# One transposing transfer for both 16-bit planes of a tile, and other due times for the weights' transfers

## The chip, the cores and the metric

The kernel runs on one core of a Trainium2 chip. Its time is the device time of the program in microseconds. Before the change it is 1276.15 us, the median of three runs (1275.52 to 1277.26).

## What is computed

Two layers of a hybrid block over 272 tokens (16 learned ones and 256 of the input) with 1024 features, all in fp32, and a norm at the end:

```python
for li in range(DEPTH):
    h = h + mixer(rms_norm(h, norm_mix_g[li]), w_in[li], w_branch[li], w_out[li], ...)
    h = h + conv_ffn(rms_norm(h, norm_ffn_g[li]), w_ffn_in[li], ...)
h = rms_norm(h, norm_final_g)

def mixer(hn, ...):
    proj = hn @ w_in                      # 1024 -> 13312 columns, split into 12 parts
    o_ret = retention(rq, rk, rv, rg)     # 4 heads, keys of 128, values of 256
    o_hg = hgrn2(hq, hf, hi, hg)          # 8 heads, gated linear recurrence
    o_da = diff_attention(dq, dk, dv)     # 8 heads, difference of two softmaxes
    y = sum(sigmoid(gate_n) * (branch_n @ w_branch[n]) for n in range(3))
    return y @ w_out
```

The padding of 112 positions that the reference puts ahead is left out by the kernel, since no valid token sees it.

## The kernel before, in words

**Products.** Activations lie with features on partitions and tokens along the row. Every weight tile of 128x128 is the stationary operand, the tokens are the moving one. For the precision of fp32 each weight tile is split into two parts, whi and wlo, and each activation into hi and lo, and three matmuls add up (L953 to L955): whi with hi, whi with lo, wlo with hi. The text calls these three one product. Parts of three outputs that are cut like this are also the operands of the heads (L1062 to L1064).

**Weights.** `_Weights.next` (L642 on) brings them in chunks of eight tiles, 512 KB: a transfer on SP's queue into `wraw` (three buffers), a copy on ACT into `whi` and a subtraction on DVE into `wlo` (four buffers each). The copy and the subtraction carry a due time, the moment at which the first product of the chunk is planned; the transfer has none.

**Turns.** Values, the maps of attention, some tails and, at the end, the residual are needed with tokens on partitions. `to_tokens`, `flip`, `da_rest` and `residual` do it without TensorE: ACT copies the upper and the lower 16 bits of each number into two planes (`apart`, for `flip` the first half of `turned`), SP issues a transposing transfer for each plane (`turned`), and ACT copies the two planes back together. A plane has one block of 128 columns in `flip`, three in `da_rest`, four in the others.

**The heads.** Retention (`ret_head`, tiles s, ro), the recurrence (`hg_heads`, `hg_outputs`, tiles lev, ho) and attention (`da_first`, `da_pair`, `da_rest`, `da_tail`, tiles ds, do) run beside the products of other parts: each is a chain over DVE, ACT, SP, GpSimd and back to TensorE. Their results on TensorE lie in two accumulators (tag "acc"). Such an accumulator comes free when the head's norm has been taken: a square on ACT, a sum over the partitions on GpSimd, a root in two steps on ACT, a multiplication on DVE.

**Order.** Every operation is recorded first (`_Engine.__getattr__`, L633 is the line of all of them), with an estimate of its cost and a key, the time at which it is wanted. `_Plan.order` then simulates the engines and writes down in which order each of them does its work; on the chip that order is fixed. At each step an engine takes the operation that can start first, and among those that can start at once the one with the lowest rank (L498 to L506): an operation whose due time is less than URGENT (3 us) behind the product that TensorE has reached goes ahead of all others, else the key decides. A transposing transfer counts as 0.06 us, plus its bytes at 360 GB/s, plus 0.7 us, and lands 2 us later.

Of the kernel before, what the change touches and what calls it, by code (L numbers as in the profile page):

```python
# [21 lines left out]
P = 128  # L22
# [17 lines left out]
SLOTS = 13  # L40
# [8 lines left out]
HOLD, PULL = 3.0, 8.0  # L49
SAFE = 1.0  # L50
SURE = 0.3
URGENT = 3


BASE = {"rq": 0, "rk": 4, "rv": 8, "rg": 16, "hq": 24, "hf": 32, "hi": 40, "hg": 48,
# [300 lines left out]
class _Plan:  # L356
# [99 lines left out]
    def order(self):  # L456
# [11 lines left out]
        held, out = set(), []  # L468
# [29 lines left out]
        def rank(op, t):  # L498
            if op.engine == "pe" and op not in mains:
                if op.fed + SAFE > t:  # L500
                    return math.inf
                return op.key - PULL if beside and op.fed + SURE <= t else op.key + HOLD
            if op.due - reached < URGENT:
                return op.due - 1000.0
            late = 8.0 if op.func in self.SETS and self.SETS[op.func] != tables else 0.0
            return op.key + late  # L506
# [4 lines left out]
        while len(out) < todo:  # L511
# [53 lines left out]
            for o in op.after:  # L565
                o.need -= 1
                if o.engine != e:
                    o.fed = max(o.fed, done + self.LAG[e])
                o.ready = max(o.ready, done + (self.LAG if o.engine != e else self.SAME)[e])
                if o.need == 0:  # L570
                    push(o)
            for o in op.then:
# [20 lines left out]
class _Engine:  # L593
# [5 lines left out]
    def __getattr__(self, method):  # L599
        f = getattr(self.engine, method)  # L600

        def call(*args, **kw):
# [20 lines left out]
            if method == "reciprocal":  # L623
                cost += 7 * self.each * n
            elif method == "tensor_tensor_scan":
                cost += self.each * n
            elif method == "transpose":
                cost = 0.11
            elif method == "matmul":
                cost = max(0.218 if args[1].shape[-1] > 32 else 0.07, 4 * n / 2400 + 0.02)  # L630
            elif method == "dma_start":
                cost = self.fixed + self.each * n * outs[0].shape[0] + (0.7 if kw.get("transpose") else 0.0)
            self.plan.add(self.name, lambda: f(*args, **kw), cost, outs, ins, kind)  # L633

        return call
# [2 lines left out]
class _Weights:  # L638
# [13 lines left out]
    def next(self):  # L652
        c, i = divmod(self.used, CHUNK_TILES)
        self.used += 1
        if i == 0:
            due = self.plan.key
            room = [P, ROOM]
            raw = self.plan.tile(self.pool, [P, CHUNK_TILES * P], F32, "wraw", 3, f"wraw{c}")
            hi = self.plan.tile(self.pool, room, F32R, "whi", 4, f"whi{c}")
            lo = self.plan.tile(self.pool, room, F32R, "wlo", 4, f"wlo{c}")  # L660
            self.plan.key = due - LEAD
            pieces = 1 if c > 1 else 2
            for p in range(pieces):
                n = CHUNK_TILES // pieces
                cols = slice(p * n * P, (p + 1) * n * P)
                self.sp.dma_start(raw[:, cols], self.w[c][:, cols])
                order, places = self.places[c]
                mine = [[x[i] for i in order[p * n : (p + 1) * n]] for x in places]
                for first, outer, inner, dims in _boxes(*mine):
                    src = self.part(raw, (p * n + first) * P, inner * P, P, outer, inner)  # L670
                    to_hi, to_lo = (self.part(t, *x, outer, inner) for t, x in zip((hi, lo), dims))
                    self.act.activation(to_hi, src, AF.Copy)
                    self.dve.tensor_tensor(out=to_lo, in0=src, in1=to_hi.bitcast(F32), op=SUB)
                    for op in self.plan.ops[-2:]:
                        op.due = due
            self.plan.key = due
            self.cut = hi, lo
        return tuple(t[:, at[i] : at[i] + P] for t, at in zip(self.cut, self.places[c][1]))
# [16 lines left out]
def _trace(ctx, tc, plan, a, depth, probe):  # L695
# [298 lines left out]
    def planes(name, n):  # L994
        return new(tp, [P, 4 * T], U16, "vsrc", 4, name)[:, : 2 * n].rearrange("p (i x) -> p i x", i=2)

    def to_tokens(src, vt, e):

        apart, turned = planes("apart", 4 * P), planes("turned", 4 * P)
# [2 lines left out]
        for i in range(2):  # L1002
            act.activation(apart[:, i].rearrange("p (c f x) -> p c f x", c=2, f=2),
                           halves(src[:, :, : 2 * P], i).rearrange("p f (c x) -> p c f x", c=2), AF.Copy)
        for i in range(2):
            sync.dma_start(turned[:, i].rearrange("p (b x) -> p b x", x=P), apart[:, i], transpose=True)
        turned = turned.rearrange("p i (c x) -> p i c x", c=2)
        if top is None:
            for i in range(2):
# [10 lines left out]
    def flip(out, x):  # L1020
# [3 lines left out]
        halves = lambda t, i: t.bitcast(U16).rearrange("p (x two) -> p x two", two=2)[:, :, i]  # L1024
        for i in range(2):
            act.activation(apart[:, i], halves(x, i), AF.Copy)
        for i in range(2):
            sync.dma_start(turned[:, i].rearrange("p (b x) -> p b x", x=P), apart[:, i], transpose=True)
        for i in range(2):
            act.activation(halves(out, i), turned[:, i], AF.Copy)  # L1030

# [46 lines left out]
    for li in range(depth):  # L1078
# [365 lines left out]
        def da_rest(b, hd, sb, nm, sm, cf, tiles):  # L1444
# [17 lines left out]
            for i in range(2):  # L1462
                for c, n, at in ((0, 2 * P, P), (T, P, 0)):
                    act.activation(apart[:, i, at : at + n], halves(w[:, c : c + n], i), AF.Copy)
            for i in range(2):
                sync.dma_start(turned[:, i].rearrange("p (b x) -> p b x", x=P), apart[:, i], transpose=True)
            for i in range(2):
                act.activation(halves(a1[:, META : T + P], i), turned[:, i], AF.Copy)

# [73 lines left out]
        def residual():  # L1543
# [5 lines left out]
            for g, (t, c) in enumerate(((0, 0), (0, 1), (1, 0))):  # L1549
                apart, turned = planes("apart", 4 * P), planes("turned", 4 * P)  # L1550
                halves = lambda x, i: x.bitcast(U16).rearrange("p k (x two) -> p k x two", two=2)[:, :, :, i]
                for i in range(2):
                    act.activation(apart[:, i].rearrange("p (k x) -> p k x", k=4), halves(h[:, 4 * c : 4 * c + 4, META + t * P : META + (t + 1) * P], i), AF.Copy)
                for i in range(2):
                    sync.dma_start(turned[:, i].rearrange("p (b x) -> p b x", x=P), apart[:, i], transpose=True)
                for i in range(2):
                    act.activation(halves(st["old"][:, g : g + 1], i), turned[:, i].unsqueeze(1), AF.Copy)
                plan.key += 20.0
# [250 lines left out]
```

## Time and profile before

| | |
|---|---|
| median of three runs | 1276.15 us |
| the profiled execution | 1276.58 us |
| its span, first to last instruction | 1274.8 us |
| TensorE busy | 1261.6 us |
| VectorE (DVE), ScalarE (ACT), GpSimd (POOL) busy | 964.8, 899.2, 115.5 us |
| weights' transfers on SP's queue | 402 of 512 KB and 4 of 256 KB |
| transposing transfers on SP's queue | 86 and 36 |

The profile is of one execution. TensorE's matmuls (PE) and weight loads (PEld) have rows of their own; SPq, ACTq and so on are the engines' sequencers, and an SPq row of a transfer is the time that SP needs to issue it, not that of the data. Releasers, in rows as `<-DVE wlo`, are inferred from semaphores: what came last before a waiting instruction could start. The parts of the program in order of time: the first layer's projections with the recurrence to about 200 us, retention to 262, attention with the three branches to 455, the feed-forward part to 651; the second layer the same way to the end.

### The profile page before, as it was taken

To read this page: it belongs to the slowest core of one execution; us is meant where nothing else is said; L and a number is where in the kernel's file an instruction comes from. 1 tells how busy PE (TensorE), PEld (TensorE's weight loads), DVE (VectorE), ACT (ScalarE), POOL (GpSimd) and SP (SyncE) were. 2 spreads that over 40 slices of the span, in tenths; PEclk is the share of its full clock that TensorE was granted. 3 is DMA by queue.
4 is the path that set the end of the run, shared out by engine and by line. 5 is a ranking of instruction groups with operands and counts; after the bars stand their busy time and mean duration, and the time that the engine had idled before them with its cause. 6 is when DMAs were issued, how large, how long until landed. Compare 5 with 4: busy or idle time off the path is not lost.

```text
span 1274.8 us, 28782 instructions
## 1 busy us (share of the span) xinstructions
PE 1261.6 (99%) x11612; PEld 1240.7 (97%) x11612; DVE 964.8 (76%) x1677; ACT 899.2 (71%) x1700; POOL 115.5 (9%) x89
## 2 busy tenths in 40 slices
PE   9999999999999999999999999999999999999998
PEld 9999999999999999999999999999999999999986
DVE  6797587899775789886576875878897868898854
ACT  6766687788797576665456567887788975787643
POOL 2000031101111000000010000411012210000000
PEclk9999999999999999999999999999999999999999
DMA  7655557556647546556555546475565566576663
GB/s 269 196 168 155 165 152 216 170 152 190 197 142 207 183 151 198 180 170 193 172 180 180 168 145 190 151 228 174 154 190 176 166 202 203 167 213 205 206 196 110
DMA packets 109205, 230.49 MB, mean 181 GB/s; under 512 B 55312, under 2 KB 55440, under 8 KB 109072
## 3 DMA queue, kind: packets, MB, share of 16 engines
q1 hardware_dynamic: 108784, 228.13, 58.0%
q8 instruction: 91, 1.49, 0.5%
q10 hardware_dynamic: 288, 0.52, 0.1%
q14 instruction: 42, 0.34, 0.1%
HBM read 216.16 MB, written 1.05 MB: 170 GB/s over the span
## 4 chain that ended last, share of the span: by engine, by line
PE 84%; issue 5%; DVE 3%; DMA 3%; ACT 3%; POOL 2%; SPq 0%; ACTq 0%; POOLq 0%; DVEq 0%
PE main L953 24%; PE main L955 24%; PE main L954 24%; DMA wraw<-in_w 3%; POOL hr L633 2%; PE fo L1593 2%; PE fo L1594 2%; PE fo L1595 2%; PE lev L1178 1%; DVE wlo L633 1%; PE fi L955 1%; PE fi L954 1%; PE fi L953 1%; ACT whi L633 1%; PE ds L1422 1%
## 5 line engine op out<-in xcount | busy, mean ns | idle before, releaser
L953 PE MATMUL main<-xh,whi 128*128 128x272 f32 (+1 forms) x2240 | 642.6, 287 | 0.7 <-ACT whi L633 0.7
L633 DVE TENSOR_TENSOR wlo<-wraw,whi 128x1024 fp32r<-128x1024 f32 (+1 forms) x411 | 498.4, 1217 | 188.6 <-ACT whi L633 183.1
L955 PE MATMUL main<-xh,wlo 128*128 128x272 f32 (+1 forms) x2240 | 636.9, 284 | 1.2 <-DVE wlo L633 1.0
L954 PE MATMUL main<-xl,whi 128*128 128x272 f32 (+1 forms) x2240 | 636.1, 284 | 1.0 <-issue 1.0
L633 ACT ACTIVATE whi<-wraw 128x1024 fp32r<-128x1024 f32 (+1 forms) x411 | 426.1, 1041 | 195.2 <-PE main L954 78.5
L955 PEld LDWEIGHTS main<-xh,wlo 128*128 128x128 f32 x2240 | 421.6, 188 | 3.5 <-DVE wlo L633 2.2
L953 PEld LDWEIGHTS main<-xh,whi 128*128 128x128 f32 x2240 | 421.7, 188 | 2.2 <-ACT whi L633 1.2
L954 PEld LDWEIGHTS main<-xl,whi 128*128 128x128 f32 x2240 | 421.7, 188 | 0.2
L633 POOL PARTITION_ALL_REDUCE hr<-hsq x36 | 76.9, 2155 | 426.6 <-ACT hsq L633 388.9
L633 DVE SCALAR_TENSOR_TENSOR two_b<-main,small,two_b 128x256 f32<-128x256 f32 (+2 forms) x128 | 54.6, 487 | 28.3 <-ACT two_b L633 28.2
L633 ACT ACTIVATE two_b<-main,small 128x272 f32<-128x272 f32 (+1 forms) x64 | 33.1, 566 | 28.1 <-PE main L955 28.1
L953 PE MATMUL main<-ghi,whi 128*128 128x272 f32 x176 | 50.8, 289 | 0.0
L954 PE MATMUL main<-glo,whi 128*128 128x272 f32 x176 | 50.6, 287 | 0.0
L955 PE MATMUL main<-ghi,wlo 128*128 128x272 f32 x176 | 50.3, 286 | 0.0
L955 PE MATMUL main<-b1hi,wlo 128*128 128x272 f32 (+1 forms) x128 | 36.6, 286 | 1.2 <-DVE wlo L633 1.2
L953 PE MATMUL main<-b0hi,whi 128*128 128x272 f32 (+1 forms) x128 | 37.3, 291 | 0.2 <-DVE y L633 0.2
L953 PE MATMUL main<-b1hi,whi 128*128 128x272 f32 (+1 forms) x128 | 37.1, 290 | 0.0
L953 PE MATMUL main<-yhi,whi 128*128 128x272 f32 (+1 forms) x128 | 36.4, 284 | 0.0
L955 PE MATMUL main<-yhi,wlo 128*128 128x272 f32 (+1 forms) x128 | 36.3, 284 | 0.0
L954 PE MATMUL main<-b0lo,whi 128*128 128x272 f32 (+1 forms) x128 | 36.3, 284 | 0.0
L954 PE MATMUL main<-b1lo,whi 128*128 128x272 f32 (+1 forms) x128 | 36.3, 284 | 0.0
L954 PE MATMUL main<-ylo,whi 128*128 128x272 f32 (+1 forms) x128 | 36.3, 284 | 0.0
(283 smaller groups left out, 2169.2 us busy)
## 6 DMA issues: line engine op xcount, KB each, us to landing
wraw<-in_w SPq DMA_DIRECT2D x402, 512.0 KB, 3.8
turned<-apart SPq DMA_TRANSPOSE x86, 2.7
h<-in_h SPq DMA_DIRECT2D x4, 272.0 KB, 5.6
dec<-in_dec SPq DMA_DIRECT2D x2, 544.0 KB, 6.1
wraw<-in_w SPq DMA_DIRECT2D x4, 256.0 KB, 5.2
const<-in_const SPq DMA_DIRECT2D x1, 937.0 KB, 5.4
turned<-turned SPq DMA_TRANSPOSE x36, 2.4
gain<-in_gl SPq DMA_DIRECT2D x1, 512.0 KB, 5.0
```

The source lines that it names most:

```text
L633: self.plan.add(self.name, lambda: f(*args, **kw), cost, outs, ins, kind)
L953: nc.tensor.matmul(o, wh, hi, start=first, stop=False)
L954: nc.tensor.matmul(o, wh, lo, start=False, stop=False)
L955: nc.tensor.matmul(o, wl, hi, start=False, stop=last)
L1178: nc.tensor.matmul(o, keys, x, start=True, stop=True)
L1422: nc.tensor.matmul(ss[m][:, at : at + nk], q[half, hd, q0 : q0 + P], k[half, hd, :nk], start=True, stop=True)
L1593: nc.tensor.matmul(o, gh, wh, start=first, stop=False)
L1594: nc.tensor.matmul(o, gl, wh, start=False, stop=False)
L1595: nc.tensor.matmul(o, gh, wl, start=False, stop=end)
```

## The change

1. The two transfers of a turn become one, in a function `turn`: planes and blocks are one list of blocks, twice as long (8, 6 or 2 instead of 4, 3 or 1).
2. The planner counts a turn as 1.3 us, whatever its size, and lets it start no sooner than half a us (STILL) after its planes are written.
3. The weights' transfers get the due time of their chunk (from the 14th on), and URGENT becomes a number for each engine: 4.5 us for ACT, 3 as before for DVE, 12 for SP, where it puts the weights ahead of turns.

```diff
-URGENT = 3
+URGENT = {"act": 4.5, "dve": 3.0, "sp": 12.0}
+TURN = "turn"
+STILL = 0.5
...
-            if op.due - reached < URGENT:
+            if op.due - reached < URGENT.get(op.engine, 0.0):
                 return op.due - 1000.0
...
-                o.ready = max(o.ready, done + (self.LAG if o.engine != e else self.SAME)[e])
+                o.ready = max(o.ready, done + (self.LAG if o.engine != e else self.SAME)[e] + STILL * (o.func == TURN))
...
             elif method == "dma_start":
-                cost = self.fixed + self.each * n * outs[0].shape[0] + (0.7 if kw.get("transpose") else 0.0)
+                cost, kind = (1.3, TURN) if kw.get("transpose") else ( self.fixed + self.each * n * outs[0].shape[0], None)
...
                 self.sp.dma_start(raw[:, cols], self.w[c][:, cols])
+                fetch = self.plan.ops[-1]
...
                     for op in self.plan.ops[-2:]:
                         op.due = due
+                    fetch.due = due if c > SLOTS else math.inf
...
+    def turn(out, x):
+
+        sync.dma_start(out.rearrange("p i (b x) -> p (i b) x", x=P), x.rearrange("p i x -> p (i x)"), transpose=True)
...
-        for i in range(2):
-            sync.dma_start(turned[:, i].rearrange("p (b x) -> p b x", x=P), apart[:, i], transpose=True)
+        turn(turned, apart)
```

The last piece stands in `to_tokens`, `flip`, `da_rest` and `residual`. The order moves on all engines; TensorE does the same matmuls, with the heads' products at other places among the main ones. Three places follow, each before and after.

SP, second layer, the end of attention. The transfers into wraw are weights, turned_1882 is a turn of the last head, turned_1889 that of the tails. Before:

```order
L633 DMA wraw_1999<-in_w 128x1024
L633 DMA wraw_2002<-in_w 128x1024
L633 DMA_TRANSPOSE turned_1882<-apart_1881 128x3x128
L633 DMA_TRANSPOSE turned_1889<-turned_1889 128x1x128 x2
L633 DMA_TRANSPOSE turned_1882<-apart_1881 128x3x128
L633 DMA wraw_2006<-in_w 128x1024
L633 DMA wraw_2009<-in_w 128x1024
```

After:

```order
L635 DMA wraw_1999<-in_w 128x1024
L635 DMA_TRANSPOSE turned_1874<-apart_1873 128x6x128
L635 DMA wraw_2002<-in_w 128x1024
L635 DMA_TRANSPOSE turned_1889<-turned_1889 128x2x128
L635 DMA wraw_2006<-in_w 128x1024
L635 DMA_TRANSPOSE turned_1882<-apart_1881 128x6x128
L635 DMA wraw_2009<-in_w 128x1024
```

Four transfers stood ahead of wraw_2006 behind wraw_2002, now one does; turned_1874, the turn of the head before, has moved down to here.

ACT, second layer, the start of the second half of attention. two_a and two_b are the two maps of a pair of heads (1840 and 1841 of the one, 1842 and 1843 of the other), whi_1960 the split of a chunk of weights. Before, the end of the stretch between the copy wts_1830 and that split:

```order
L633 ACTIVATE two_b_1843,dm_1845<-two_b_1843,dm_1845 128x272
L633 ACTIVATE two_a_1842,dm_1845<-two_a_1842,dm_1845 128x144
L633 ACTIVATE apart_1847<-two_a_1840 128x256
L633 ACTIVATE apart_1847<-two_a_1840 128x128
L633 ACTIVATE apart_1847<-two_a_1840 128x256
L633 ACTIVATE apart_1847<-two_a_1840 128x128
L633 ACTIVATE dt_1834<-two_a_1840 128x16 x2
L633 ACTIVATE m_957_1932<-main_1940 128x2x258
L633 ACTIVATE two_b_1843,dm_1845<-two_b_1843,dm_1845 128x144
L633 ACTIVATE whi_1960<-wraw_1959 128x4x256
```

After:

```order
L635 ACTIVATE whi_1952<-wraw_1951 128x1024
L635 ACTIVATE wts_1830<-turned_1832 128x128
L635 ACTIVATE whi_1960<-wraw_1959 128x4x256
L635 ACTIVATE two_a_1840,dm_1844<-two_a_1840,dm_1844 128x272
L635 ACTIVATE two_b_1841,dm_1844<-two_b_1841,dm_1844 128x272
L635 ACTIVATE two_a_1840,dm_1844<-two_a_1840,dm_1844 128x144
```

The split now stands ahead of all eight exponentials and of the planes (apart_1847).

ACT, first layer, retention. sum_484 and hr_485 are the squares and the root of head 0's norm, tw_473 the tails that its second product waits for, whi_563 and whi_566 splits of weights. Before:

```order
L633 ACTIVATE tw_473<-ro_472 128x128
L633 ACTIVATE whi_554<-wraw_553 128x1024
L633 ACTIVATE kt_490<-wts_489 128x272
L633 ACTIVATE sum_484<-ro_482 128x272
L633 ACTIVATE sum_484<-ro_483 128x272
L633 ACTIVATE whi_563<-wraw_562 128x1024
L633 ACTIVATE vsrc_546<-main_535 128x544
L633 ACTIVATE whi_566<-wraw_565 128x1024
L633 ACTIVATE hr_485<-hr_485,eps_84 128x272
```

After:

```order
L635 ACTIVATE tw_473<-ro_472 128x128
L635 ACTIVATE whi_554<-wraw_553 128x1024
L635 ACTIVATE kt_480<-wts_479 128x272
L635 ACTIVATE kt_490<-wts_489 128x272
L635 ACTIVATE whi_563<-wraw_562 128x1024
L635 ACTIVATE sum_484<-ro_482 128x272
L635 ACTIVATE sum_484<-ro_483 128x272
L635 ACTIVATE vsrc_546<-main_535 128x544
L635 ACTIVATE apart_547<-vsrc_546 128x512 x2
L635 ACTIVATE hr_485<-hr_485,eps_84 128x272
```

The two splits have left the stretch between squares and root, and two planes have come into it.

On TensorE, counted in products of the main stream: head 0's second products of that retention (ro_482, ro_483) stand behind product 554 instead of 550, head 1's behind 570 as before; in the second layer's attention do_1875 stands behind 2465 instead of 2444, do_1883 behind 2482 instead of 2477.

More of the change, by code (lines that the diff above doesn't have):

```diff
@@ L1026, in flip @@
             act.activation(apart[:, i], halves(x, i), AF.Copy)
-        for i in range(2):
-            sync.dma_start(turned[:, i].rearrange("p (b x) -> p b x", x=P), apart[:, i], transpose=True)
+        turn(turned, apart)
         for i in range(2):
@@ L1464, in da_rest @@
                     act.activation(apart[:, i, at : at + n], halves(w[:, c : c + n], i), AF.Copy)
-            for i in range(2):
-                sync.dma_start(turned[:, i].rearrange("p (b x) -> p b x", x=P), apart[:, i], transpose=True)
+            turn(turned, apart)
             for i in range(2):
@@ L1553, in residual @@
                     act.activation(apart[:, i].rearrange("p (k x) -> p k x", k=4), halves(h[:, 4 * c : 4 * c + 4, META + t * P : META + (t + 1) * P], i), AF.Copy)
-                for i in range(2):
-                    sync.dma_start(turned[:, i].rearrange("p (b x) -> p b x", x=P), apart[:, i], transpose=True)
+                turn(turned, apart)
                 for i in range(2):
```

## The prediction

> **What bounds the kernel now.** I read the page first: the busy shares, the slices, the chain that ended last, and the median landing of a chunk of weights.
>
> ```profile
> span 1274.8 us, 28782 instructions
> PE 1261.6 (99%) x11612; PEld 1240.7 (97%) x11612; DVE 964.8 (76%) x1677; ACT 899.2 (71%) x1700; POOL 115.5 (9%) x89
> PE 84%; issue 5%; DVE 3%; DMA 3%; ACT 3%; POOL 2%; SPq 0%; ACTq 0%; POOLq 0%; DVEq 0%
> wraw<-in_w SPq DMA_DIRECT2D x402, 512.0 KB, 3.8
> ```
>
> TensorE is busy for 99% of the span. The change takes no matmul away, so it can save only time in which TensorE stands still. The windows view says where it does not. Columns: stretch, length, then busy time with the count of instructions for PE, PEld, DVE, ACT and POOL, then clock, DMA share and GB/s.
>
> ```profile
> 395.00:665.00 270.00, 270.00 (x2191) 270.00 (x2190) 201.81 (x301) 166.13 (x243) 6.90 (x11) 1.00 0.57 181
> 1032.00:1205.00 173.00, 173.00 (x1480) 173.00 (x1480) 145.71 (x233) 127.52 (x195) 4.27 (x3) 1.00 0.65 200
> ```
>
> From 395 to 665 and from 1032 to 1205 us TensorE is never idle, and nothing can be won there. These rows also price one product (a weight tile, three matmuls): 3 x 270 / 2191 = 0.370 us in the first layer and 3 x 173 / 1480 = 0.351 us in the second. What is left are the mixers, 145 to 1032 us without that stretch. There I asked for the waits of the weight loads (PEld), since a load that waits stops the matmuls behind it. Each row: who waited, for whom, us in total, times, longest. The last row is of 900 to 1032 us alone, the second layer's attention.
>
> ```profile
> PEld main L955 <- DVE wlo L633: 2.8, 4, 1.0
> PEld ro L1062 <- issue: 1.5, 2, 1.0
> PEld main L955 <- issue: 1.1, 1, 1.1
> PEld do L633 <- PE main L955: 0.5, 1, 0.5
> PEld ro L1062 <- ACT tw L633: 0.5, 1, 0.5
> PEld main L953 <- ACT whi L633: 0.5, 1, 0.5
> PEld do L1063 <- DVE near L633: 0.4, 2, 0.3
> PEld main L953 <- issue: 0.4, 1, 0.4
> PEld do L633 <- DVE da L633: 0.2, 1, 0.2
> PEld do L1062 <- issue: 0.2, 1, 0.2
> ...
> PEld main L955 <- DVE wlo L633: 2.1, 3, 1.0
> ```
>
> The ten sum to 8.1 us, all that the change can win: 0.6% of the span. Of it 2.8 + 0.5 = 3.3 us are waits for split weights, 2.1 + 0.5 of them in the second layer's attention. Retention (ro, all of the first layer) has 2.0, the heads of attention (do) 1.3, a branch's start 0.4. The 1.1 us has no releaser and stands at 733 us among the recurrence's rounds, where the order does not change; I leave it.
>
> **The transfers.** The view of the tile "turned" gives min/median/max of an issue in ns, then what ACT waited for, then us to landing.
>
> ```profile
> L633 SPq DMA_TRANSPOSE turned<-apart x86: 1178/1234/2645, 120.1 to 1154.1; - x86
> L633 SPq DMA_TRANSPOSE turned<-turned x36: 1100/1176/1914, 131.8 to 1019.0; - x36
>   DMA turned<-apart: 7.8, 7
>   DMA turned<-turned: 6.1, 5
> DMA to landing us min/median/max: 2.2/2.5/6.2
> ```
>
> A turn of one block of 128 columns (turned<-turned) holds SP for 1.176 us, one of three or four blocks for 1.234. Three more blocks cost about 0.06 us; eight blocks are then about 1.31 us (an estimate from these two rows). Before, 86 x 1.234 + 36 x 1.176 = 148 us of SP; after, 43 x 1.31 + 18 x 1.20 = 78 us. SP gets 70 us back, which is worth nothing by itself: it pays only where a chunk of weights is queued behind a turn and is late. The data of a turn is unchanged. The second plane used to land 1.27 + 2.5 = 3.8 us after the pair began; now both land after about 2.6. ACT's first copy comes 0.1 us later, its second 1.2 us earlier. The issue of the merged form is not in this trace: it lies between 1.18 us (size costs nothing) and 2.47 us (two of the old ones). I take 1.31, near the lower end, because the step from one block to four is so small, and keep 2.47 for a rival. The half us of STILL and the due times act through the order alone; no instruction on the chip gets a new wait by them.
>
> [...]
>
> **The weights, second layer: -2.6 us.** The largest wait is at 1027 to 1029 us. What TensorE waited for at its end, and SP's queue ahead of it:
>
> ```profile
> 1028.80 0.39 PE L955 MATMUL main<-xh,wlo 128*128 128x258 f32 x1 [0.76 <-DVE wlo L633]
> ```
>
> ```profile
> 1016.67 3.40 SPq L633 DMA_TRANSPOSE turned<-turned  x2
> 1020.12 1.25 SPq L633 DMA_TRANSPOSE turned<-apart  x1
> 1021.47 9.51 SPq L633 DMA_DIRECT2D wraw<-in_w  x5
> ```
>
> And the split on DVE that frees the buffer of the first of these chunks:
>
> ```profile
> 1015.37 1.22 DVE L633 TENSOR_TENSOR wlo<-wraw,whi 128x1024 fp32r<-128x1024 f32 x1
> ```
>
> Chunk wraw_2006 starts at 1021.47, behind three turns that hold SP from 1016.67. Its buffer (three are in turn) was read for the last time by the split that ends at 1016.6, so it could start 4.9 us earlier. The new order puts it ahead of turned_1882 and behind one merged turn: at least 1.25 us (the last turn) plus 1.2 us (the pair become one) earlier, against waits of 0.5 us for whi and at most 1.0 for wlo. They go.
>
> The other is at 988.4 us, and there it is ACT.
>
> ```profile
> 972.92 0.33 SPq L633 DMA_DIRECT2D wraw<-in_w  x1
> ...
> 979.47 0.56 ACT L633 ACTIVATE wts<-turned 128x128 uint16<-128x128 uint16 x2 [2.17 <-DMA turned<-turned]
> 985.70 1.05 ACT L633 ACTIVATE whi<-wraw 128x1024 fp32r<-128x1024 f32 x1
> ```
>
> Chunk wraw_1959, issued at 972.92, is in place by 979 or so (3.8 us to landing in the median, and two chunks are ahead of it), and ACT was idle for 2.17 us until 979.47. Yet its split starts at 985.70, behind eight exponentials and the planes of a head. The new order has it right behind the first copy of the turn, some 5.5 us earlier; the softmax behind it starts 1.05 us later, and its turn with it. That fits with where most of the second layer's heads now stand on TensorE, 4 to 21 products later. It costs nothing as long as the last head is done before the third branch needs its second half.
>
> ```profile
> 1037.95 1.24 DVE L633 TENSOR_TENSOR b2lo<-da,b2hi 128x1032 fp32r<-128x1032 f32 x1 [0.35 <-ACT b2hi L633]
> ...
> 1039.88 0.28 PE L953 MATMUL main<-b2hi,whi 128*128 128x258 f32 x1
> ```
>
> That half was split by 1039.2 us, and TensorE came to it eight products after 1039.88, at 1042.7: 3.5 us of cover. The last head moves 5 products, 1.75 us. The cover shrinks to about 1.7 us, and beyond it each us is paid in full.
>
> **The weights, first layer: -0.7 us.** The one wait left of the 2.8, at 379.7 us, is a chunk's split that stands on DVE behind the split of a branch:
>
> ```profile
> 377.19 1.28 DVE L633 TENSOR_TENSOR b2lo<-da,b2hi 128x1088 fp32r<-128x1088 f32 x1
> 378.39 1.21 DVE L633 TENSOR_TENSOR wlo<-wraw,whi 128x1024 fp32r<-128x1024 f32 x1
> ```
>
> The new order has this chunk ahead of the branch, 1.3 us earlier against a wait of 0.7.
>
> **Retention, first layer: 2.0 us become 1.2.** Head 0's second product waited 0.5 us for tw, which follows a turn; it now stands four products (1.5 us) later. But head 1 needs head 0's accumulators: between them stood 20 products, 7.4 us, and still 1.0 us was lost; now 16 stand there, 5.9 us. On the other side, ACT no longer has a weight split between the squares and the root. I take 0.8 us as the gain, from 2.0 (both gone) to -1.0.
>
> **The other waits: 1.7 us become 0.8.** Five for the operands of attention's heads (1.3) and one for a branch's (0.4). Later positions on TensorE give their operands more time, new neighbours take some; about half is a choice.
>
> **New waits: +1.3 us.** The order moves at more than 30 places, and the old one lost its 8.1 us in fourteen waits of about 0.6 us. The likeliest: do_1875 now stands 21 products later and only 17 products (6.0 us) ahead of do_1883, which takes its accumulator. That release took, from the first read to the last, 1013.85 to 1019.7 us:
>
> ```profile
> 1013.85 0.17 ACT L633 ACTIVATE dot<-do 128x32 f32<-128x32 f32 x1
> ...
> 1019.27 0.47 DVE L633 SCALAR_TENSOR_TENSOR da<-do,subg,hr 128x242 f32<-128x242 f32 x1 [0.69 <-ACT hr L633]
> ```
>
> That is 5.9 us, with nothing to spare. I keep 0 to 4 us for the term.
>
> **Sum.** -2.6 - 0.7 - 0.8 - 0.9 + 1.3 = -3.7 us. The profiled execution took 1276.6 us (1.8 around its span), so it would take 1272.9; the median of the timed runs is 0.4 lower, and the forecast is 1272.5 us.
>
> **Rivals.** (1) All waits of the mixers go and none comes: -7.0 us, 1269.2. For it: 70 us of SP and later heads. Against: the accumulators above, which no transfer frees. (2) No change: the weights' 3.3 us go, but the later heads give them back at accumulators, -0.5 us, 1275.6. For it: retention's 20 products became 16, and do_1883's spare is nothing. Against: in the second layer retention's heads stood 16 to 20 products apart in the old order, and the rows have no ro wait there. (3) Slower: the merged turn costs by its blocks, 2.47 us. The new order counts on 1.3, so each turn's copies, and the head's products behind them, come 1.2 us late. The waits above show five head products that start the moment their operand is there; at 1.2 us each, with the weights' 3.3 us still won, that is +2.7 us, 1278.8. It decides from an issue of about 2.0 us (five times 0.66 equals the 3.3). Against: the rows of 1176 and 1234 ns. [...] (4) The order is not what it says: the printed order has 61 turns and weights ahead of them, so I give it nothing.
>
> **Chances.** Forecast (1270.5 to 1273.6) 0.48, (1) 0.12, (2) 0.28, (3) 0.12. A measurement of this kernel tells about 0.2%, 2.6 us, from no change. Faster by more: 0.60; within: 0.28; slower: 0.12. The range, 1269.5 to 1277.5, leaves out part of (1) and most of (3).
>
> **What would show it.** Right: turned issues near 1.3 us, 61 of them; no wait for wlo or whi after 145 us; PEld waits of the mixers at 3 to 4 us with the 1.1. Wrong: issues near 2.4 us; waits for wlo that moved rather than went; ro or do waiting over 1 us for accumulators; a wait ahead of the second half of the third branch near 1040 us.

## The result, and the profile after

The changed kernel takes **1282.42 us** (median of four runs, 1281.18 to 1283.60) against 1275.86 us of the kernel before in runs beside it (1275.52 to 1277.26): 1.0055 times as long, with an interval of 1.0042 to 1.0068. It is slower, and above the range. The profiled execution took 1283.6 us. From its page: the span, the busy shares, the chain, the all-reduce of the heads' norms, and the median landing of the weights and of the turns.

```profile
span 1281.8 us, 28712 instructions
PE 1264.9 (99%) x11612; PEld 1242.1 (97%) x11612; DVE 964.5 (75%) x1677; ACT 896.5 (70%) x1700; POOL 125.2 (10%) x89
PE 72%; issue 8%; DVE 7%; ACT 6%; DMA 4%; POOL 3%; SPq 0%; DVEq 0%; ACTq 0%; POOLq 0%
L635 POOL PARTITION_ALL_REDUCE hr<-hsq x36 | 85.4, 2395 | 427.4 <-ACT hsq L635 408.2
wraw<-in_w SPq DMA_DIRECT2D x402, 512.0 KB, 3.7
turned<-apart SPq DMA_TRANSPOSE x43, 4.0
```

ACT and DVE are no busier than before. The chain has moved: TensorE has 72% of it instead of 84%, and the difference went to DVE, ACT, DMA, POOL and to waits without a releaser. The work of the heads has come onto the path.

The tile "turned", in the view that was quoted of before:

```profile
L635 SPq DMA_TRANSPOSE turned<-apart x43: 1209/1232/1813, 120.2 to 1161.5; - x43
L635 SPq DMA_TRANSPOSE turned<-turned x18: 1167/1180/1917, 129.6 to 1018.1; - x18
  DMA turned<-apart: 12.9, 12
  DMA turned<-turned: 5.7, 3
DMA to landing us min/median/max: 2.3/4.0/6.2
```

The issue is what was forecast, even a little less: six or eight blocks (the row has both) hold SP for 1.232 us. The data is not: it lands 4.0 us after the issue began, not 2.6. ACT stood still for turns 18.6 us (12.9 + 5.7) instead of 13.9.

The waits of the weight loads in the mixers, here from 145 to 1045 us:

```profile
PEld ro L1068 <- issue: 2.0, 2, 1.5
PEld main L959 <- DVE wlo L635: 2.0, 2, 1.2
PEld ds L1428 <- DVE da L635: 1.9, 2, 1.6
PEld do L635 <- DVE tw L635: 1.5, 2, 1.2
PEld main L957 <- ACT whi L635: 1.0, 1, 1.0
PEld do L1068 <- issue: 0.8, 1, 0.8
PEld main L958 <- issue: 0.7, 1, 0.7
PEld do L1069 <- DVE near L635: 0.7, 2, 0.4
PEld ho L1068 <- issue: 0.5, 1, 0.5
PEld do L1068 <- ACT kt L635: 0.5, 1, 0.5
PEld do L1068 <- DVE da L635: 0.3, 1, 0.3
PEld ro L1068 <- PE main L958: 0.2, 1, 0.2
```

They sum to 12.1 us; before it was 8.1. And the feed-forward part, which was never idle before, now loses 1.4 us (160.00 - 158.55) with the turns of the residual in it:

```profile
1045.00:1205.00 160.00, 159.30 (x1350) 158.55 (x1349) 133.97 (x215) 114.60 (x177) 2.71 (x1) 1.00 0.64 195
```

Together 4.0 + 1.4 = 5.4 of the 7.0 us by which the span grew; where the other 1.6 us lie these rows do not say.

What grew most among ACT's waits in the mixers is not the wait for turns. First the kernel before, then after: the root of a head's norm (hr), waiting for the all-reduce on GpSimd.

```profile
ACT hr L633 <- POOL hr L633: 14.9, 17, 2.4
```

```profile
ACT hr L635 <- POOL hr L635: 27.2, 22, 3.1
```

One place shows what follows from such a wait. After the change, second layer, end of attention, start and length in us:

```profile
1016.02 5.04 POOL L635 PARTITION_ALL_REDUCE hr<-hsq  x1 [9.24 <-DVE two_a L635]
...
1021.09 0.50 ACT L635 ACTIVATE hr<-hr,eps 128x242 f32<-128x242 f32 x1 [3.06 <-POOL hr L635]
...
1022.78 1.03 ACT L635 ACTIVATE whi<-wraw 128x1024 fp32r<-128x1024 f32 x1
...
1023.86 0.39 PE L957 MATMUL main<-xh,whi 128*128 128x258 f32 x1 [0.78 <-ACT whi L635]
...
1025.39 0.39 PE L959 MATMUL main<-xh,wlo 128*128 128x258 f32 x1 [1.02 <-DVE wlo L635]
```

ACT stands 3.06 us for the all-reduce, has the rest of the root and two copies of turned tiles next in its order, and only then splits the chunk that TensorE needs. That chunk, wraw_1999, had landed at 1016.88. The wait for wraw_2006, which was to go, is gone; this one has come in its stead.

### The profile page after: what moved, and what is told of

Its sections match the earlier page's. It is cut to its first block, busy times and chain, and to the rows that moved or that the text cites. A ratio compares the mean times of both kernels' runs of the same rounds, so it can differ in the third digit from the quotient of the medians.

```text
span 1281.8 us, 28712 instructions
## 1 busy us (share of the span) xinstructions
PE 1264.9 (99%) x11612; PEld 1242.1 (97%) x11612; DVE 964.5 (75%) x1677; ACT 896.5 (70%) x1700; POOL 125.2 (10%) x89
## 3 DMA queue, kind: packets, MB, share of 16 engines
q8 instruction: 91, 1.49, 0.5%
HBM read 216.16 MB, written 1.05 MB: 169 GB/s over the span
## 4 chain that ended last, share of the span: by engine, by line
PE 72%; issue 8%; DVE 7%; ACT 6%; DMA 4%; POOL 3%; SPq 0%; DVEq 0%; ACTq 0%; POOLq 0%
PE main L957 21%; PE main L958 20%; PE main L959 20%; POOL hr L635 3%; DVE wlo L635 2%; ACT whi L635 2%; DMA wraw<-in_w 2%; PE fo L1597 2%; PE fo L1598 2%; PE fo L1599 2%; DMA turned<-apart 1%; PE lev L1184 1%; DVE two_b L635 1%; DVE two_c L635 1%; PE fi L957 1%
## 5 line engine op out<-in xcount | busy, mean ns | idle before, releaser
L635 POOL PARTITION_ALL_REDUCE hr<-hsq x36 | 85.4, 2395 | 427.4 <-ACT hsq L635 408.2
L635 ACT ACTIVATE hr<-hr,eps 128x272 f32<-128x272 f32 (+4 forms) x44 | 21.7, 498 | 27.5 <-POOL hr L635 27.2
L635 POOL PARTITION_ALL_REDUCE sum<-sum x3 | 7.5, 2496 | 308.0 <-DVE sum L635 308.0
```

## The experiments

All are the changed kernel (or, where said, the kernel before) with one thing edited. "Planned" is how long after the start of a turn's issue the planner counts on its data: before, 2 x 1.49 + 2.0 = 5.0 us for the second of two planes with four blocks (the formula of L632, which counts four bytes for each number, though a plane's numbers have two); after, 1.3 + 2.0 = 3.3 us. What the planner counts beyond the time that the data really takes is called slack. "ACT for turned" is its idle time in the view of the tile; "ACT for hr" and the sum of the PEld waits are those of the mixers. All in us; ratios are to the kernel before, with their intervals.

| run | planned | landing, median | ACT for turned | ACT for hr | PEld waits | time | ratio |
|---|---|---|---|---|---|---|---|
| before | 5.0 | 2.5 each | 13.9 | 14.9 | 8.1 | 1275.86 | 1 |
| after | 3.3 | 4.0 | 18.6 | 27.2 | 12.1 | 1282.42 | 1.0055 [1.0042, 1.0068] |
| e1 | order of before | 3.1 | 29.6 | 12.7 | 6.3 | 1277.59 | 1.0025 [1.0013, 1.0038] |
| e2 | 3.3 | 3.1 each | 12.5 | 27.2 | 12.7 | 1280.83 | 1.0048 [1.0030, 1.0067] |
| e3 | 5.0 | 3.8 | 0 | 16.9 | 2.3 | 1270.72 | 0.9969 [0.9955, 0.9984] |
| e4 | 3.3 | 3.6 | 16.2 | 23.7 | 7.0 | 1278.92 | 1.0029 [1.0017, 1.0042] |
| e5 | 4.3 | 3.6 | 1.0 | 25.8 | 4.4 | 1272.48 | 0.9981 [0.9970, 0.9993] |
| e6 | 3.3 | 3.7 | 15.6 | 16.2 | 4.8 | 1281.95 | 1.0048 [1.0032, 1.0065] |
| e7 | 5.0 | 3.1 each | 0.7 | 19.0 | 5.5 | 1273.02 | 0.9982 [0.9972, 0.9991] |
| e8 | 5.0 | 3.2 | 0.6 | 17.1 | 5.7 | 1274.95 | 0.9997 [0.9987, 1.0007] |
| e9 | 3.3 | 3.5 | 8.6, none at a copy | 26.9 | 11.7 | 1282.82 | 1.0062 [1.0047, 1.0078] |
| e10 | 3.8 | 3.5 | 5.2 | 20.5 | 5.4 | 1275.29 | 1.0001 [0.9992, 1.0010] |
| e11 | 5.0 | 3.9 | 0 | 8.3 | 2.8 | **1269.41** | 0.9960 [0.9946, 0.9974] |
| e12 | 3.3 | 3.5 | 14.5 | 25.7 | 7.5 | 1278.40 | 1.0029 [1.0018, 1.0040] |
| e13 | 3.3 | 3.6 | 14.1 | 13.1 | 3.2 | 1273.35 | 0.9986 [0.9974, 0.9998] |
| e14 | 3.3 | 3.6 | 19.0 | 17.1 | 6.9 | 1278.83 | 1.0031 [1.0014, 1.0047] |
| e15 | 6.0 | 2.6 each | 4.3 | 21.4 | 7.7 | 1275.50 | 1.0003 [0.9993, 1.0013] |
| e16 | 5.0 | 3.6 | 0 | 3.5 | 2.2 | 1269.72 | 0.9960 [0.9945, 0.9975] |
| e17 | 5.0 | 2.5 each | 11.2 | 5.4 | 7.8 | 1277.52 | 1.0025 [1.0011, 1.0038] |
| e18 | 5.0 | 3.9 | 0.9 | 13.5 | 3.5 | 1271.99 | 0.9971 [0.9961, 0.9981] |

### The transfer, the order and the price apart: e1 to e4

**e1**: the order of before on every engine, with the two transfers of a turn joined behind the planner, at the place of the second (or just ahead of the first reader of either plane, where that comes earlier).

```diff
         order = [None] + self.order()
+        for both, run in self.pairs:
+            a, b = sorted(both, key=order.index)
+            order.remove(a)
...
+            b.run = run
```

> The order of the kernel before on ACT, DVE, POOL and TensorE, and its weights on SP in the same order, but one transfer for both planes of a turn, at the place of the second. Theory A (the loss comes from the new order, the merged transfer itself is harmless): 1274 to 1276 us, no slower than before, since the landing of the merged transfer, 4.0 us in the median after the change, is about that of the old second plane (1.27 + 2.5 us or later). Theory B (the merged transfer lands too late for the copies that wait for it): 1279 us or more, most of the 6.5 us.

**e2**: the order of after on every engine, with two transfers at each turn.

```diff
-        sync.dma_start(out.rearrange(...), x.rearrange(...), transpose=True)
+        def run():
+            for i in range(2):
+                nc.sync.dma_start(out[:, i].rearrange("p (b x) -> p b x", x=P), x[:, i], transpose=True)
+
+        plan.add("sp", run, 1.3, [out...], [x...], TURN)
```

> The changed kernel's order on every engine, but each turn issued as two transfers, one behind the other, at the place of the one. Theory A (order): 1282 us or slower, up to 1286, since SP is held 1.2 us longer at each of 61 places and the order was planned for 1.3 us. Theory B (the merged transfer): back to 1276 to 1278 us.

**e3**: after, with the planner's old price of the pair for the one transfer.

```diff
-                cost, kind = (1.3, TURN) if kw.get("transpose") else ( self.fixed + self.each * n * outs[0].shape[0], None)
+                cost, kind = self.fixed + self.each * n * outs[0].shape[0], None
+                if kw.get("transpose"):
+                    cost, kind = cost + self.fixed + 1.4, TURN
```

> The changed kernel, but the planner counts a turn as dear as the old pair (2.9 us for four blocks instead of 1.3). Due times, URGENT and STILL stay. Theory A1 (inside the order, it is the low price: 1.3 us + 2.0 us to landing planned, 4.0 us measured, so that copies and head products are placed too early): 1275 to 1278 us. Theory A2 (it is the due times and URGENT): 1281 us or more.

**e4**: after, with the old rule of due times.

```diff
-URGENT = {"act": 4.5, "dve": 3.0, "sp": 12.0}
+URGENT = {"act": 3.0, "dve": 3.0, "sp": 3.0}
...
-                    fetch.due = due if c > SLOTS else math.inf
+                    fetch.due = math.inf
```

> The changed kernel with one transfer a turn, the price of 1.3 us and STILL, but URGENT 3 for all engines and no due time for the weights' transfers. Theory A1 (the price): 1281 us or more. Theory A2 (due times and URGENT): 1275 to 1278 us.

Measured: 1277.59, 1280.83, **1270.72** and 1278.92 us. The one transfer in the old order costs 0.25%. ACT waits longer for turns, since the first plane now comes with the second (29.6 us instead of 13.9), but TensorE's loads in the mixers wait no longer than before (6.3 us against 8.1), so what the 0.25% is made of stays open:

```profile
  DMA turned<-apart: 23.0, 16
  DMA turned<-turned: 6.6, 3
```

But the loss of the changed kernel is in its order: with two transfers again (e2) it is nearly all there. And of the order it is mostly the price: with the old one (e3), due times, half a us and one transfer as in the change, the kernel is faster than both. In e3 ACT never waits for a turn, and TensorE's loads wait 2.3 us in the mixers.

### What in the price: e5, e6, e10 and e11

A price of 1.3 instead of 2.98 us changes two things: how long SP is held in the plan, and when the data is counted on. **e5**, **e10** and **e11** keep 1.3 us for SP and put the landing 1.0, 0.5 and 1.7 us later; **e6** does the opposite (the old price for SP, and `late` takes the landing back).

```diff
             for o in op.after:
+                late = 1.0 * (op.func == TURN)
                 o.need -= 1
                 if o.engine != e:
-                    o.fed = max(o.fed, done + self.LAG[e])
+                    o.fed = max(o.fed, done + self.LAG[e] + late)
-                o.ready = max(o.ready, done + (self.LAG if o.engine != e else self.SAME)[e] + STILL * (o.func == TURN))
+                o.ready = max(o.ready, done + (self.LAG if o.engine != e else self.SAME)[e] + STILL * (o.func == TURN) + late)
```

> The planner keeps the changed kernel's price of a turn for SP (1.3 us) but counts on its data 1.0 us later (4.3 us after the planned start instead of 3.3; the changed kernel's trace has 4.0 us from issue to landing in the median). Theory (consumers of turns are placed too early, because the plan lands them too early): ACT's idle time for turned falls from 18.6 us to under 5, the mixers' PEld waits from 12 us to 3 to 6, and the time to 1270 to 1275 us. Rival S (what mattered is how long SP is held in the plan: with 1.3 us SP's transfers are packed too tightly): no gain, 1279 to 1284. Rival L (any other order gives some time between 1271 and 1283 by chance): no relation, ACT's idle time for turned stays above 10 us.

> The opposite half: the planner holds SP for a turn as long as for the old pair (2.9 us for four blocks), but counts on its data as early as the changed kernel does (3.3 us after the planned start). Theory (landing): no better than the changed kernel, 1278 to 1284 us, ACT idle for turned above 10 us. Rival S (SP's hold): near the 1270.7 us of the kernel with the whole old price, 1269 to 1273, ACT idle for turned under 5 us.

> As e5 with half the amount: the planner counts on a turn's data 3.8 us after its planned start (3.3 in the changed kernel, 4.3 in e5; measured 3.6 to 4.0 in the median). Theory (landing): between the two, 1273 to 1279, ACT's idle time for turned between 1 and 18.6 us, say 4 to 10. Rival L (each order gives its own time by chance): any time from 1271 to 1283, with no relation to ACT's idle time.

> As e5 with more: 5.0 us after the planned start, as long as the old plan counted for the second plane. Theory: no ACT wait for turned is left to win beyond e5's 1.0 us, and the time stays within 1270 to 1274. Rival L: any time from 1271 to 1283.

Measured: 1272.48 (e5), 1281.95 (e6), 1275.29 (e10), 1269.41 (e11). Planned landings of 3.3, 3.8, 4.3 and 5.0 us give 1282.4, 1275.3, 1272.5 and 1269.4, all with the short hold of SP. A later landing alone is enough for the whole gain. The long hold alone (e6) gains nothing, but one order does not clear it: in the mixers TensorE's loads wait 4.8 us, about as little as in e5, and the largest loss is a single place, the one that the prediction had named as a cover that could run out, the second half of the third branch (it falls behind 1045 us, outside the column of the table):

```profile
PEld main L960 <- ACT b2hi L638: 5.4, 1, 5.4
```

The tile "turned" in e11: the data lands as late as after the change, and nobody waits for it (the view has no row of ACT waiting for the transfer).

```profile
L636 SPq DMA_TRANSPOSE turned<-apart x43: 1209/1231/1887, 120.0 to 1147.3; - x43
L636 SPq DMA_TRANSPOSE turned<-turned x18: 1167/1184/2057, 130.9 to 1015.0; - x18
DMA to landing us min/median/max: 2.3/3.9/6.2
```

And all the PEld waits of its mixers, four instead of twelve rows:

```profile
PEld main L958 <- issue: 1.1, 1, 1.1
PEld ro L1069 <- ACT tw L636: 0.7, 1, 0.7
PEld ho L1069 <- PE main L960: 0.6, 1, 0.6
PEld main L960 <- issue: 0.4, 1, 0.4
```

### What carries the gain of e3: e7 and e8

**e7** is e3's order with two transfers at each turn (the edit of e2), **e8** is e3 with the old rule of due times (the edit of e4).

> The order of e3 (whole old price in the planner, 1270.7 us), each turn issued as two transfers again. It tells what the merged transfer itself is worth in an order whose plan is right. If the merging is what made e3 fast: back to 1274 to 1277 us, with waits of ACT for the second plane. If it is the order (due times, weights ahead of turns, turns half a us later): 1269 to 1272, the same as e3 within 0.2%. In the old order the merged transfer cost 0.25% and in the changed kernel's order 0.12%, so a loss of e3 against this one, 1268 to 1269.5, is possible too.

> As e3 (merged transfer, old price in the planner, half a us of STILL), but with the old URGENT of 3 us for all engines and no due time for the weights' transfers. If the due times carry e3's gain: 1274 to 1277 us, with waits for wlo of 2 to 3 us back. If the honest price carries it: 1269 to 1273. With the wrong price the due times cost about 0.25% (1278.9 without them against 1282.4), so they may not help here either.

Measured: 1273.02 and 1274.95 us. The due times may carry 4.2 us of e3's gain, and the one transfer 2.3; but the intervals of e3 and e7 overlap, and a shuffle of the order can move as much (e12), so neither is settled by one run. Under the short price the due times gained nothing: without them the kernel is 3.5 us faster (e4).

### Is it the wait for the data? e9

The order of after, instruction for instruction, and the same transfers; ACT's copies read a constant instead of the turned tile.

```diff
-                act.activation(halves(vt[:, :, e : e + 2 * P], i), turned[:, i], AF.Copy)
+                act.activation(halves(vt[:, :, e : e + 2 * P], i), turned[:, i], AF.Copy, real=(None, stand(turned[:, i])))
```

(`real` holds the operands that the instruction gets on the chip, the others those of the plan; the other copies in the same way. The copies that wrote into apart, which the transfer reads, write into the source tile.)

> The changed kernel's order on every engine, instruction for instruction, and the same transfers; but ACT's copies out of a turned tile read a constant instead, so that no copy waits for a transfer to land (the transposition is thereby left out of what is computed). Theory (the copies stand too close behind their transfers, and ACT, DVE, GpSimd and TensorE wait behind them): ACT's idle time for turned goes from 18.6 us to 0, most of the mixers' PEld waits of 12 us with it, 1269 to 1275 us. Rival O (the order is bad in itself: heads' products close to their accumulators, weights behind other work): no or little gain, 1279 to 1283 us.

Measured: 1282.82 us, no gain, and PEld waits of 11.7 us. **My theory fell here** in the form in which it stood, that the time is lost where the copies wait. The run is not as clean as I had expected: of the 14.6 us that ACT waited for turns in the mixers 8.6 remain, at six places where it writes new values or planes into a buffer whose turn is still under way. But in the attention of both layers, from 281 to 400 and from 918 to 1045 us, none of these is left, and there TensorE's loads still wait 7.0 us instead of 8.8. The first layer shows why. After the change, ACT and DVE:

```profile
324.39 1.13 ACT L635 ACTIVATE wts<-turned 128x384 uint16<-128x384 uint16 x2 [1.19 <-DMA turned<-apart]
...
328.10 1.18 DVE L635 TENSOR_TENSOR tw<-tails,const 128x128 f32<-128x128 f32 x1
```

In e9:

```profile
322.69 1.12 ACT L641 ACTIVATE wts<-const 128x384 uint16<-128x384 uint16 x2
...
325.80 1.06 ACT L641 ACTIVATE whi<-wraw 128x1024 fp32r<-128x1024 f32 x1 [1.52 <-DMA wraw<-in_w]
...
328.03 1.18 DVE L641 TENSOR_TENSOR tw<-tails,const 128x128 f32<-128x128 f32 x1
```

The copy comes 1.7 us earlier, and the tw that TensorE waits for comes only 0.07 us earlier: the next entry but one in ACT's order is a weight split whose chunk has not landed, and tw stands on DVE behind the subtraction that belongs to it. Here, in a fixed order, the time won at one entry was lost at the next one that was late. The waits for the all-reduce are still there too, 26.9 us.

### What the slack had covered: e13, e14, e16

The planner prices the all-reduce of 242 to 256 columns at 1.7 to 1.8 us (0.2 plus 6.3 ns per column); the pages have 2.155 us before and 2.395 after, as means of 36, of which four have only 128 columns; the other 32 take 2.27 and 2.53 us in the mean. The price is about that of the shortest (1.76 us with 242 columns). **e13** prices this alone; **e16** is e13 and e11 together.

```diff
-                cost, kind = 0.2 + 6.3e-3 * n, method
+                cost, kind = 0.9 + 6.3e-3 * n, method
```

**e14** keeps every price and sets SAFE from 1.0 to 2.0, which holds back the heads' products on TensorE and touches no price.

> The changed kernel, a turn still priced 1.3 us and its data counted on 3.3 us after the planned start; only the all-reduce on GpSimd is priced 0.7 us higher in the planner (0.9 instead of 0.2, plus 6.3 ns per column: 2.4 to 2.5 us for 242 to 256 columns; the changed kernel's page has 2395 ns, the planner had 1.7 to 1.8). Theory R (the long price of a turn had covered other underpriced steps of a head's chain, this one first): half or more of the loss comes back, 1271 to 1277 us, and ACT's idle time for hr falls from 27 us to under 15. Theory landing alone: 1278 to 1284.

> The changed kernel with SAFE at 2.0 instead of 1.0: TensorE's products of the heads are put at least 2 us behind the planned readiness of their operands, whatever engine makes these; all prices stay. Theory P (the short landing costs because TensorE's own products of the heads stand too early): 1269 to 1275 us, the mixers' PEld waits under 6 us. If it costs through the queues of ACT and DVE instead: 1278 to 1284. As no price is touched, a gain would also say that e5 and e11 gained through TensorE's positions.

> e11 (a turn's data 5.0 us after the planned start, 1269.4 us) together with the all-reduce's price of e13. If the two stand in for each other (slack is slack): no more than e11, 1268.5 to 1271. If each covers its own shortfall: 1266.5 to 1268.5.

Measured: **1273.35** (e13), 1278.83 (e14), 1269.72 (e16). The price of an operation with no part in the change takes back 9.1 us, while ACT still waits for turns as long as before the change:

```profile
  DMA turned<-apart: 13.6, 11
  DMA turned<-turned: 0.5, 1
```

Its wait for the all-reduce is halved:

```profile
ACT hr L635 <- POOL hr L635: 13.1, 10, 2.7
```

At the place that was shown at 1016 to 1025 us the all-reduce is as long as it was there (5.08 us), and no wait of TensorE for whi or wlo follows: a copy now stands ahead of the root, and the split right behind it.

```profile
1007.36 5.08 POOL L635 PARTITION_ALL_REDUCE hr<-hsq  x1 [9.25 <-ACT hsq L635]
...
1009.84 0.63 ACT L635 ACTIVATE wts<-turned 128x384 uint16<-128x384 uint16 x1
1012.48 0.50 ACT L635 ACTIVATE hr<-hr,eps 128x242 f32<-128x242 f32 x1 [2.01 <-POOL hr L635]
1012.88 1.04 ACT L635 ACTIVATE whi<-wraw 128x1024 fp32r<-128x1024 f32 x1
```

With both corrections nothing is added (e16 against e11): each can stand in for the other. e14's ten runs lie anywhere from 1273.92 to 1283.38 us, so it says only that a distance on TensorE alone is no full cure.

### Chance, and the kernel before: e12, e18, e15, e17

**e12** and **e18** shuffle an order for no reason that has to do with turns: SAFE at 1.05 in the changed kernel, at 1.1 in e11. **e15** counts on each plane 1.0 us later in the kernel before (the edit of e5), **e17** prices the all-reduce there (that of e13).

> The changed kernel with SAFE at 1.05 instead of 1.0: 93 of TensorE's rows and 100 of ACT's change places for no reason that has to do with turns; price and landing stay 1.3 and 3.3 us. Theory: it stays as slow as the changed kernel, 1278 to 1284, ACT's idle time for turned above 10 us. Rival L: any time from 1271 to 1283, as likely below 1277 as above.

> e11 (a turn's data 5.0 us after the planned start, 1269.4 us) with SAFE at 1.1 instead of 1.0, which makes about a hundred of TensorE's rows and of ACT's change places. Theory (planned landing sets the level): 1268 to 1273, as e12 stayed slow with its 1278.4. Rival L (chance): any time from 1269 to 1282.

> The kernel before, two transfers a turn, with each plane's data counted on 1.0 us later than the 2.0 us behind its planned issue; nothing else. If slack alone makes a kernel of this family faster: 1269 to 1272 us, and the gain of e11 belongs to the slack and not to the change. If the kernel before already had enough (5.0 us planned for the second plane, 3.8 measured from the start of the pair): 1274 to 1277.

> The kernel before, two transfers a turn and its old prices, with only the all-reduce priced as in e13. If the long price of the pair had already covered the all-reduce in the old plan: 1273 to 1277 us, within 0.2% of before (ACT's idle time for hr was 14.9 us there against 27.2 in the changed kernel, so at most some of that is to be won). If the all-reduce's price alone makes any kernel of this family fast: 1269 to 1272 us, and the merged turn would be worth nothing in itself.

Measured: 1278.40, 1271.99, 1275.50 and 1277.52 us. A shuffle is worth 4.0 and 2.6 us, so a step of that size between two runs here says little. The groups stand apart all the same: the short landing with the old price of the all-reduce gives 1278.4 to 1282.8 in seven runs, and the new due times with slack in either form 1269.4 to 1273.4 in seven; e10, with a landing 0.5 us later, and e8, with the old due times, lie between. The kernel before gains from neither form, and with the all-reduce's price it is 0.25% slower (e17), though ACT's wait for the all-reduce falls from 14.9 to 5.4 us there. I read this as slack enough in its old price, 5.0 us for data that came in 3.8.

## Why the prediction was wrong, point by point

- **What bounds the kernel** held in the main: 4.0 of the 7.0 us by which the span grew are PEld waits of the mixers. Another 1.4 came in the feed-forward part, where nothing could be won but, as it shows, something lost. That new ones can come was in the text, as one of the five terms, +1.3 us.
- **The transfers: this step failed.** The issue was right (1.232 us for 1.31, so that SP got its 70 us). The landing was not: "both land after about 2.6" came from the 2.5 us of one plane plus the longer issue. It was 4.0. About half a us of this is the size: among the turns of three or more blocks a plane that had no weights' transfer still under way ahead of them when SP had issued them, the median went from 2.48 to 3.06 us. The rest goes with company on the queue: with one such transfer under way it was 4.14, with two 5.42, and 30 of these 43 turns now have one or two, against 47 of 86. In the order of before (e1) it was 21 of 43; with the old due times in the new order (e4) it is still 28, so that the weights' new rank on SP explains little of it.
- **The same step read the price as SP's alone.** The 1.3 us also say when the planner counts on the data: 3.3 us instead of 5.0, against a landing of 4.0. "The half us of STILL and the due times act through the order alone" was true and was then priced from three places of the order. The plan's slack per turn went from +1.2 to -0.7 us (5.0 - 3.8 and 3.3 - 4.0), and the slack had been paying for other steps as well, the all-reduce among them (e13).
- **Weights, -3.3 us forecast: -0.3 came.** The waits at 379.7 and 988.4 us are gone. So is that for wraw_2006, whose transfer starts at 1019.47 instead of 1021.47. But 3.0 us came at other chunks, 2.2 of them (1.0 for whi, 1.2 for wlo) at wraw_1999, whose data was there 5.9 us before ACT came to split it. This is "waits for wlo that moved rather than went", as the text had it for the case that it was wrong: I had looked at SP's order and not at what stands ahead of the split on ACT.
- **Retention in the first layer, 2.0 to 1.2 forecast: 1.5.** Head 0's wait for tw is gone, and so is one of 0.4; head 1's is 1.5 us instead of 1.0, behind 16 products instead of 20, and is for the accumulators (the matmul at 243.58 us waits 1.35 us for DVE's ho, the multiplication that frees them). The other 0.7 us of ro came in the second layer, which had no such wait before.
- **The other waits, 1.7 to 0.8 forecast, and new ones, +1.3: here is the loss.** The heads of attention (do, ds) wait 5.7 us instead of 1.3, and the feed-forward part 1.4 instead of 0. The place that I had priced, do_1883, cost 0.3, and the second half of the third branch nothing: the places were named from the few rows that I had compared, the loss was spread over a dozen others.
- **The rivals.** The third had the right mechanism, copies and products that come late against a plan that counts on 1.3 us, and the nearest time, 1278.8. It was given 0.12 because it was tied to the issue ("decides from an issue of about 2.0 us"), which the rows excluded. It should have been tied to the landing. No run shows its term, a merged issue of 2.47 us: six or eight blocks took 1.232 us against 1.234 for three or four.

What is shown: counting on a turn's data later, and nothing else, takes the whole loss back and more (e5, e10, e11), 13.0 us in e11, while the two shuffles moved the time by 4.0 and 2.6 us (e12, e18); slack at another step of a head's chain does most of the same (e13, e16); the same slack does nothing for the kernel before (e15, e17). What is not: whether a longer hold of SP would have gained too, had the third branch not lost its cover (e6); how much the half us of STILL does, which no run takes out by itself (e11 has it and is the fastest); and which single wait carries the loss. e9 takes away the copies' waits without gain (and leaves others for buffers), e5 gains with 25.8 us of waits for the all-reduce, e13 gains with 14.1 us of waits for turns. I read this as a loss by the sum of the lateness at successive entries of ACT's and DVE's orders; no run isolates that.

## What to carry to other kernels

Where a planner orders the work, a price is also a promise to everything behind the operation: before correcting one, ask which other steps its error was paying for, and read the landing of the data, not only the issue. Taking a wait out of a fixed order (e9) tells whether the time is lost there; pricing an unrelated step (e13) did what that did not. When such a kernel is changed, a shuffle with no meaning should be run beside it, since it moved this one by up to 4 us.

## What the runs showed of the hardware

SP issued a transposing transfer of six or eight blocks in 1.232 us and one of three or four in 1.234: the longer list was free at the issue, and cost 0.6 us at the landing (3.06 us against 2.48, both with no weights' transfer still under way ahead).

An all-reduce of 242 to 272 columns took from 1.76 to 5.04 us before and after the change (up to 5.08 in e13), one of 128 columns from 1.07 to 1.41. The longest one after the change, from 1016.02 to 1021.06, ran beside three subtractions in a row on DVE:

```profile
1015.94 1.22 DVE L635 TENSOR_TENSOR wlo<-wraw,whi 128x1024 fp32r<-128x1024 f32 x1
1017.08 1.23 DVE L635 TENSOR_TENSOR b2lo<-da,b2hi 128x1032 fp32r<-128x1032 f32 x1
1018.22 1.22 DVE L635 TENSOR_TENSOR wlo<-wraw,whi 128x1024 fp32r<-128x1024 f32 x1
```

Whether these made it long the trace does not settle. The two shortest of 242 columns after the change took 1.76 us each, one (at 1005.03 us) with 0.37 us of DVE beside it, the other (at 970.16 us) with DVE beside it all along, and one of 2.88 us had only 1.16 us of DVE beside it. Over the 40 of 242 columns and more, the correlation of length and DVE time beside it is 0.61 before the change and 0.58 after, but a longer one has room for more beside it in any case: with the share of its length that DVE was busy the correlation is 0.10 and -0.02. The profile's legend calls GpSimd's spans rough, too.
